# Row factors of an encoder layer's groups through memory, with TensorE's first microseconds laid out anew

## The chip, the cores and the metric

The kernel runs on one core of a Trainium2 chip. Its five engines run side by side and each takes its own instructions strictly in order: TensorE (PE) multiplies matrices, VectorE (DVE) and ScalarE (ACT) work elementwise, GpSimd (POOL) does slower elementwise work, and SyncE (SP) issues the DMA transfers, which 16 DMA engines carry out. The metric is the device time of the program in microseconds, smaller being better. The kernel before took 1175.03 us, the median of three runs (1173.93 to 1175.19).

## The reference

One hybrid encoder layer on x (4096 tokens, 1024 channels, float32):

```python
h = rmsnorm(x, pre_norm_g)                    # row factor = rsqrt(mean(x*x) + eps)
proj = einsum('bsd,de->bse', h, w_in)         # 1024 x 2304: q | k | v | g_a | u_p | g_p
a = banded_attention(q, k, v, rel_bias, sink) * silu(g_a)     # |i - j| <= 128
p = multiscale_pool(u_p, pool_w, pool_scale) * silu(g_p)
mixed = concat([a, p]) @ w_out
x = x + rmsnorm(mixed, post_norm_g)
```

The part that matters here is the first line: every token has one factor, and every channel of that token is multiplied by it before the projection. The bias of the attention is a table (32 buckets, 8 heads) that is spread over 512 relative positions.

## The kernel before

The work has two stages. Stage A (0 to about 500 us of the span) makes the gates and the pooled values (g_p, u_p, g_a); stage B makes q, k, v, the attention and the output. Float32 products are carried by pairs of float16 numbers: each operand is split in a high part (ACT copies it to float16) and a low part (DVE subtracts), and a product is three float16 matmuls.

Stage A handles the 4096 tokens in eight groups of 512, m = 0 to 7. Channels lie on the partitions, tokens along the free dimension, so a token's factor has to stand on all 128 partitions. For a group m the steps are (`prepare`, from line 933): four loads of x by token, four squares with row sums on ACT (`square`, L316), the power -1/2 on POOL (`root`, L304), which leaves the factors as a tile `rs` of 128 x 4; then on TensorE `spread_all` (L413): four float32 matmuls of `rs` against the identity, after which the factor of token t stands in column t of the PSUM tile `bc` on every partition. For each of four channel pairs the transposed x is loaded into `nt`, DVE multiplies it with `gsc` and `bc` (`norm`, L307), ACT and DVE split the result into `xb` and, for sums of quarters, `xt` (L446, L464, L304). The products (`y`, `x`, `v`, L634) follow; each result leaves its PSUM bank through an ACT copy (L742, L740) and a DVE addition (`cc`, `ubuf`).

Group 0 has a path of its own at the start of the kernel, for which the rest waits. Its x comes channel-major in 16 loads of 128 KB (`xb<-in_xT`, rows of 1 KB), for its first 256 tokens u = 0 and then for u = 1. ACT squares the four chunks of u = 0 (L387), DVE adds them up, TensorE sums over the partitions (`first_sum`, L398, into `sp`), DVE and POOL make the factors, TensorE spreads them (`bc`, L413), and DVE multiplies (`xb<-xb,gsc,bc`, L307). Beside it DVE needs the largest gain (`gain_most`; `gain_spread`, L370, on TensorE; the chain from L374 to `gh`), and the first weights need their column norms: ACT squares a weight tile (L519), TensorE sums it (`w_norm`, `n2ga` and `n2gb`, L528), DVE turns that into scales (`w_scale`, seven short instructions from L188), and ACT and DVE split the weights (L557, L307 `wq`). Only then do the products `plain` start: for half the channels with weight quarter A11, then A12, then for the other output half A21 and A22.

In stage A the order on every engine is set by a planner, `Steps.run`. A step has an engine, an estimated duration, a due time (`key`), the keys it reads and writes, and an assumed DMA time. The planner plays the steps through with these estimates: at each point it takes, on the engine that can start first, the ready step with the smallest due time. The result is a fixed order; on the chip nothing is reordered. So an edit to one step's due time or keys can move many others. Stage B has an order written out by hand, with times of its own (`plan`).

Attention's bias row is made once at about 267 us: `row_load` (two small DMAs), `row_prod` (a 32 x 512 float32 matmul, `fp`, L1009), `row_keep` (a DVE copy, L1013), `row_store`, and `bias_rows`, which spreads it through DRAM.

Of the kernel before, what the change touches and what calls it, by code (L numbers as in the profile page):

```python
# [17 lines left out]
P = 128  # L18
# [3 lines left out]
T = 512  # L22
# [34 lines left out]
class Steps:  # L57
# [28 lines left out]
    def run(self):  # L86
# [9 lines left out]
        free = dict.fromkeys(("PE", "DVE", "ACT", "POOL", "SP"), 0.0)  # L96
# [38 lines left out]
def hybrid_layer(ctx: ExitStack, tc, io, out):  # L135
# [40 lines left out]

    f_row = dram.tile([NH, 512], F32, name="f_row")
# [32 lines left out]
    with ExitStack() as actx:  # L210
# [12 lines left out]
        rs4 = pa.tile([P, 4], F32, name="rs4")  # L223
        xn1 = pa.tile([P, D], F32, name="xn")
# [115 lines left out]
        n0 = flat32(XB1).rearrange("p (k b t) -> p k b t", k=HK, b=2)  # L340
# [5 lines left out]
        for u in range(2):  # L346
            for c in range(HK):
                for b in range(2):
                    ld(-9 + 5 * u + 0.1 * c, n0[:, c, b, tok(u)], xT[c][:, b, 0, tok(u)], 0.13,
                       w=[f"n0.{c}.{u}.{b}"])  # L350
            if u == 0:
                ld(-8.75, g_pre, io["g_pre"], 0.02, w=["gpre"])
                ld(-8.74, ident, io["ident"], 0.06, w=["ident"])
            for i in range(2):
                w_load(GP, 2 * u + i, -8 + 5 * u)
# [24 lines left out]
        do("PE", 0.3, -6, gain_spread, r=["ident", "gmost"], w=["bc"])  # L380
# [5 lines left out]
        def first_square(c):  # L386
            A.activation(xsq[:, c], n0[:, c, :, tok(0)], AF.Square, scale=X_SQ)  # L387
# [34 lines left out]

        def n_view(m, c):
            if m == 0:
                return n0[:, c]
            return NT[:, (c % 2) * D : (c % 2 + 1) * D].rearrange("p (b t) -> p b t", b=2)

        def norm(m, c, b, ts=slice(0, T)):
            n = n_view(m, c)[:, b, ts]
            k = HK * b + c  # L430
            stt(n, n, gsc[:, k : k + 1], bc[m][:, ts], ALU.mult, ALU.mult)

        def norm_half(c, u):
            for b in range(2):
                norm(0, c, b, tok(u))
# [5 lines left out]
        def b_in(m, c, u=None):  # L441
            n = n_view(m, c)
            return n.rearrange("p b (u t) -> p b u t", u=2) if u is None else n[:, :, tok(u)]
# [4 lines left out]
        def b_low(m, c, u=None):  # L448
            tt(V, b_out(m, c, 1, u), b_in(m, c, u), b_out(m, c, 0, u), ALU.subtract)
# [26 lines left out]
        do("PE", 0.9, -4, first_sum, r=["onesf", "xsq3"], w=["wup1"])  # L476
# [6 lines left out]
        for u in range(2):  # L483
# [3 lines left out]
            for c in range(HK):  # L487
                do("DVE", 0.85, k + 0.5 * c, norm_half, c, u,
                   r=["gs"] + [f"bc{i}" for i in (2 * u, 2 * u + 1)]
                   + [f"n0.{c}.{u}.{b}" for b in range(2)],  # L490
# [3 lines left out]
                do("DVE", dve(512), k + 0.5 * c + 0.2, b_low, 0, c, u,  # L494
# [107 lines left out]
        norms([13, 13], 13, [tile_view(GP, i) for i in (2, 3)], [tile_keys(GP, i) for i in (2, 3)],  # L602
# [14 lines left out]
        do("DVE", 0.2, 20, gp_gates, r=["swga", "swgb"], w=["gates"])  # L617
        do("DVE", 1.2, 40, gp_flags, r=["swga", "swgb", "gates"], w=["flags", "swgc"])
        plain_weights(GP, (sw[:, 0:1], sw[:, 2:3]), ("ga", "gb"), (9.5, 12.5, 16.0, 17.0))
# [312 lines left out]

        def prepare(m):
# [7 lines left out]
            do("POOL", 1.0, key + 3, root, m, slice(0, 4), r=[f"ssq{m % 2}.{i}" for i in range(4)] + ["mhalf"],  # L941
               w=["rs4", "rs0", "rs1"])
            do("PE", 1.2, key + 5, spread_all, m, r=["rs4", "ident"], w=[f"wup{m % 2}"])
            for c in range(HK):
# [4 lines left out]
                for h in range(2):  # L949
                    do("DVE", dve(512), k + h, norm, m, c, h, r=["gs", f"wup{m % 2}"], w=[n])  # L950
# [48 lines left out]
        row_t = {}  # L999

        def row_load():
            row_t["b"] = pa.tile([32, NH], F32, name="rbias")
            nc.sync.dma_start(row_t["b"], io["rel_bias"])
            row_t["o"] = sqt[0].bitcast(F32)[:32]
            nc.sync.dma_start(row_t["o"], io["onehot"])

        def row_prod():
            row_t["p"] = psa.tile([NH, 512], F32, name="fp", tag="n20")
            nc.tensor.matmul(row_t["p"], row_t["b"], row_t["o"], start=True, stop=True)  # L1009

# [13 lines left out]
        def row_steps(key):  # L1024
            do("SP", 0.9, key, row_load, w=["row", "sqt0"], dma=0.3)
            do("PE", 1.8, key + 5, row_prod, r=["row", "sqt0"], w=["rowp", "n20"])
            do("DVE", 0.7, key + 8, row_keep, r=["rowp"], w=["n20", "rows", "sqt1"])
            do("SP", 0.45, key + 10, row_store, r=["rows", "sqt1"], w=["frow"], dma=0.1)
            do("SP", 0.45, key + 20, bias_rows, r=["frow"], w=["fscr"], dma=4.0)
# [1065 lines left out]
```

## Time and profile before

| | |
|---|---|
| time, median of 3 runs | 1175.03 us |
| time of the profiled execution | 1174.91 us |
| its span (first to last instruction) | 1172.8 us |
| PE busy | 1149.0 us (98%) |
| DVE busy | 930.8 us (79%) |
| ACT busy | 702.6 us (60%) |
| POOL busy | 309.3 us (26%) |
| DMA moved | 224.65 MB, mean 192 GB/s |

The profile was taken in one execution. A busy time is a sum over the span, and an engine that is busy all the time in one stage and idle in another has the same share as one that is half busy throughout, so the stretches are read one by one. In the timeline rows a group of like instructions has its start, the time until the last one's end, and behind the bracket the idle time ahead of it with what ended that. Matmuls are pipelined: a row's time holds the tail of its last matmul, so the distance to the next row's start is what the engine was occupied.

### The profile page before, as it was taken

Reading aid. Unit: us, or ns where it says so; the run is one execution under the profiler, and the core shown is the slowest. Engines: PE = TensorE matmul, PEld = TensorE weight load, DVE = VectorE, ACT = ScalarE, POOL = GpSimd, SP = SyncE. Lnnn points to the kernel's source line nnn. Section 1 sums busy time; section 2 is a strip of 40 time slices with the busy share of each in tenths; the row PEclk is TensorE's granted clock in tenths of the full one; section 3 lists DMA queues with packets and bytes.
Section 4 is the critical chain, followed back from the end, with each engine's and each line's share of the span. In section 5 each row is a group of like instructions: output and inputs, shape, how many; then the busy total and the mean of one; then the engine's idle time right before and its main releaser. Section 6 shows DMA issues by size and latency. Waiting matters only on the chain.

```text
span 1172.8 us, 33945 instructions
## 1 busy us (share of the span) xinstructions
PE 1149.0 (98%) x14304; PEld 883.4 (75%) x14304; DVE 930.8 (79%) x1865; ACT 702.6 (60%) x1459; POOL 309.3 (26%) x310
## 2 busy tenths in 40 slices
PE   5999999999999999999999999999999999999997
PEld 4998888888888888986667667576676667767653
DVE  6889997868788984558878878877887787887787
ACT  5875565546655552256676666666667666666672
POOL 0002111101101100201434434433533443443331
PEclk9999999999999999999999999999999999999999
DMA  8645488666756565299976886786777678687695
GB/s 315 218 111 169 162 261 268 185 234 221 255 189 232 153 186 176 56 279 209 263 184 140 191 198 133 197 196 159 182 193 185 142 190 200 136 194 160 164 234 144
DMA packets 292441, 224.65 MB, mean 192 GB/s; under 512 B 210704, under 2 KB 251920, under 8 KB 287680
## 3 DMA queue, kind: packets, MB, share of 16 engines
q1 hardware_dynamic: 292288, 222.48, 69.8%
q8 instruction: 112, 1.84, 0.6%
q14 instruction: 41, 0.34, 0.1%
HBM read 113.37 MB, written 60.33 MB: 148 GB/s over the span
## 4 chain that ended last, share of the span: by engine, by line
PE 50%; DVE 1%; ACT 0%; issue 0%; DVEq 0%; POOLq 0%; ACTq 0%
PE ms L1588 13%; PE aq L1227 12%; PE m L1588 9%; PE s L1272 4%; PE kv L1373 3%; PE o L1438 3%; PE kv L1227 3%; PE p L1438 2%; PE z L1560 1%; PE s L1560 0%; DVE pn L1336 0%; DVE mo L1627 0%; DVE p L1295 0%; ACT pn L1328 0%; DVE xt L1649 0%
## 5 line engine op out<-in xcount | busy, mean ns | idle before, releaser
L634 PEld LDWEIGHTS <-wq 128*128 128x128 f16 x4104 | 401.5, 98 | 52.7 <-issue 2.8
L634 PE MATMUL y<-xt,wq 128*128 128x256 f16 x1512 | 204.2, 273 | 0.9 <-ACT cc L742 0.9
L1306 ACT ACTIVATE p<-p,nm 128x385 f32<-128x385 f32 (+1 forms) x256 | 152.8, 599 | 35.0 <-POOL p L1289 20.3
L1227 PE MATMUL aq<-xb,xb 128*128 128x256 f16 x1024 | 173.4, 273 | 0.1
L1588 PE MATMUL ms<-wo,ys 128*128 128x512 f16 x720 | 162.7, 379 | 0.1
L1336 DVE SCALAR_TENSOR_TENSOR pn<-p,rd,pn 128x384 f16<-128x384 f32 (+1 forms) x256 | 156.1, 660 | 6.8 <-ACT pn L1328 6.8
L1295 DVE CUSTOM_DVE_ANT_0 p<-s,nt,nsink 128x384 f32<-128x384 f32 (+1 forms) x256 | 155.9, 665 | 1.8 <-PE s L1272 1.7
L1227 PEld LDWEIGHTS <-xb 128*128 128x128 f16 x1280 | 125.1, 98 | 22.8 <-issue 6.6
L1227 PE MATMUL aq<-xb,xt 128*128 128x256 f16 x512 | 139.6, 273 | 0.1
L1328 ACT ACTIVATE pn<-p,rd 128x384 f16<-128x384 f32 (+1 forms) x256 | 134.4, 596 | 4.2 <-issue 1.1
L1588 PEld LDWEIGHTS <-ys 128*128 128x128 f16 x720 | 69.2, 98 | 81.4 <-issue 2.8
L304 POOL TENSOR_TENSOR yt<-yt,sg 128x512 f32<-128x512 f32 (+2 forms) x32 | 48.0, 1499 | 311.4 <-DVE yt L307 293.1
L1588 PE MATMUL m<-wo,y 128*128 128x512 f16 x540 | 121.8, 379 | 0.0
L1588 PEld LDWEIGHTS <-y 128*128 128x128 f16 x540 | 51.5, 98 | 62.9 <-issue 2.9
L1622 POOL TENSOR_TENSOR mo<-mo,gpost 128x512 f32<-128x512 f32 x39 | 63.8, 1635 | 94.7 <-ACT jkb L1611 93.5
L634 PE MATMUL plain<-xb,wq 128*128 128x256 f16 x576 | 68.8, 276 | 3.0 <-ACT xb L446 1.8
L1227 PEld LDWEIGHTS <-xt 128*128 128x128 f16 x640 | 62.6, 98 | 8.3
L634 PE MATMUL y<-xb,wq 128*128 128x256 f16 x504 | 68.8, 273 | 0.0
L634 PE MATMUL v<-xb,wq 128*128 128x256 f16 x504 | 68.6, 273 | 0.2 <-DVE cc L304 0.2
L634 PE MATMUL v<-xt,wq 128*128 128x256 f16 x504 | 68.6, 273 | 0.0
L634 PE MATMUL x<-xb,wq 128*128 128x256 f16 x504 | 68.3, 273 | 0.0
L1272 PE MATMUL s<-k_all,q 64*32 64x288 f16 (+7 forms) x3648 | 62.5, 266 | 1.3 <-issue 1.3
(212 smaller groups left out, 1907.8 us busy)
## 6 DMA issues: line engine op xcount, KB each, us to landing
nt<-in_xT SPq DMA_DIRECT2D x28, 512.0 KB, 4.7
x_scr<-xb SPq DMA_DIRECT2D x14, 1024.0 KB, 7.2
xb<-x_scr SPq DMA_DIRECT2D x14, 1024.0 KB, 7.3
xr<-in_x SPq DMA_DIRECT2D x28, 512.0 KB, 4.6
out<-xr SPq DMA_DIRECT2D x28, 512.0 KB, 2.6
xn<-in_x SPq DMA_DIRECT2D x27, 512.0 KB, 4.4
ga_scr<-cc SPq DMA_DIRECT2D x64, 128.0 KB, 2.1
raw<-in_w_out SPq DMA_DIRECT2D x16, 512.0 KB, 5.4
```

What stands on the lines that cost most here:

```text
L304: eng.tensor_tensor(out=out, in0=in0, in1=in1, op=op)
L634: nc.tensor.matmul(b[:, s], wq[:, slot[q, op], wv, s, k, :], x[:, xv, k, :], start=(first and k + s + wv + xv == 0), stop=(last and k == H ...
L1227: nc.tensor.matmul(acc, w[:, j, k, :], x[:, kh, v, kt, :], start=(n == 0), stop=(n == 3 * KT - 1),)
L1272: nc.tensor.matmul(s_ps[qs, gg, c0:c1], q_t[u, half][a, qi, jj, tl + 32 * hq : tl + 32 * hq + 32], k_all[a, ki, kc + c0 - s0 : kc + c1 - s ...
L1295: nc.vector.tensor_tensor_reduce(out=p_t[b, half][:, hh, :nk], in0=s_t[jj][:, gg, :nk], in1=bias[:, h, lo : lo + nk], scale=negc[:, h : h ...
L1306: nc.scalar.activation(p[:, hh, : nk + 1], p[:, hh, : nk + 1], AF.Exp, bias=nm_t[b, half][:, hh : hh + 1], scale=-1.0, accum_out=den_t[b, ...
L1328: nc.scalar.activation(prob_view(b, half)[:, 0, i], p_t[b, half][:, i, :nk], AF.Copy, scale=rd_t[b, half][:, i : i + 1],)
L1336: nc.vector.scalar_tensor_tensor(out=pn4[:, 1, i], in0=p_t[b, half][:, i, :nk], scalar=rd_t[b, half][:, i : i + 1], in1=pn4[:, 0, i], op0= ...
L1373: nc.tensor.matmul(av[:, i], x[:, kh, v, kt, i * P : (i + 1) * P], w[:, B_V, k, :], start=(n == 0), stop=(n == 3 * KT - 1),)
L1438: nc.tensor.matmul(o_t[b][side][a, half], v_t[ku][ks, vi, kt, a], pt[b, half][ks, pi, g, :, kb - kbs[0], (LOW, TOP)[side]], start=start, s ...
L1588: nc.tensor.matmul(z_t[u, tag], y[:, k, yi, :], wo[o][:, wi, k, :], start=(n == 0 and acc is None), stop=(n == 3 * HK - 1), skip_group_che ...
L1622: eng.tensor_tensor(out=mo, in0=mo, in1=gpost[:, cs], op=ALU.mult)
```

## The change

Five things are changed. For the groups m = 3 to 7 the spread on TensorE is replaced: `rows_store` writes the 128 x 4 factors to 512 consecutive float32 numbers in DRAM (elements of 4 bytes), `rows_load` reads them back onto all 128 partitions as the SBUF tile `rows`, and `norm` reads that in place of `bc`; the loads, squares and the root of these groups get due times 16 us earlier, and two steps on a made-up engine "NET" tell the planner 12 and 7 us for the two transfers. The first x comes from a host-side copy `x0` in eight loads of 256 KB with rows of 2 KB. Filler matmuls (`turn_over`: `ones` times `ones`, into a bank that nobody reads) stand on TensorE: 52 ahead of `gain_spread`, 40 behind it, 24 behind the first weight scales. `first_sum` is forced ahead of the first weight norms by the key "summed". The bias row's product moves from 267 us to the start, its copy from DVE to ACT. Some steps of the first weights change their due times and keys. `LOW0` is empty, so no low part moves to POOL.

```diff
+        def row_keep():
+            row_t["s"] = row_t["o"][:NH]
+            A.copy(row_t["s"], row_t["p"])
...
+        do("SP", 0.9, -4.5, row_load, w=["row", "yt0"], dma=0.3)
+        n0 = flat32(XB1).rearrange("p (k u b t) -> p k u b t", k=HK, u=2, b=2)
...
-                for b in range(2):
-                    ld(-9 + 5 * u + 0.1 * c, n0[:, c, b, tok(u)], xT[c][:, b, 0, tok(u)], 0.13,
-                       w=[f"n0.{c}.{u}.{b}"])
+                ld(-9 + 5.5 * u + 0.1 * c, n0[:, c, u], io["x0"][u, c], 0.25, w=[f"n0.{c}.{u}"])
...
-                w_load(GP, 2 * u + i, -8 + 5 * u)
+                w_load(GP, 2 * u + i, -8 + 4 * u)
...
-        do("PE", 0.3, -6, gain_spread, r=["ident", "gmost"], w=["bc"])
+        def turn_over(n):
+            t = psa.tile([P, 2, 2 * P], F32, name=f"idle{n}", tag="v")
+            for _ in range(n):
+                nc.tensor.matmul(t[:, 0, :P], ones16, ones16, start=True, stop=True,
+                                 skip_group_check=True)
+
+        do("PE", 5.5, -9, turn_over, 52, r=["ones"], w=["bankv", "turned"])
+        do("PE", 0.3, -6, gain_spread, r=["ident", "gmost", "turned"], w=["bc", "spread0"])
+        do("PE", 2.3, -6, turn_over, 40, r=["ones", "spread0"], w=["bankv"])
...
+        def rows_store(m):
+            nc.sync.dma_start(rs_scr[m].rearrange("(i p) -> p i", i=4), rs4)
+
+        def rows_load(m):
+            bc[m] = rows
+            nc.sync.dma_start(
+                rows, rs_scr[m].rearrange("(o t) -> o t", o=1).to_broadcast([P, T])
+            )
...
-        do("PE", 0.9, -4, first_sum, r=["onesf", "xsq3"], w=["wup1"])
+        do("PE", 0.5, -4, first_sum, r=["onesf", "xsq3"], w=["wup1", "summed"])
...
-                do("PE", 0.5, key + 0.5, w_norm, z, group, i, n, b, r=["ones", f"sqt{z}"],
-                   w=[f"n2{b}"])
+                do("PE", 0.5, key + 0.5, w_norm, z, group, i, n, b,
+                   r=["ones", f"sqt{z}"] + ["summed"] * (group == "ga"), w=[f"n2{b}"])
...
+        do("PE", 1.4, 6, turn_over, 24, r=["ones", "swga"], w=["bankv"])
+        do("PE", 0.9, 5.6, row_prod, r=["row", "yt0", "summed"], w=["n20"])
+        do("ACT", 0.7, 5.6, row_keep, w=["n20", "yt0"])
+        for i, op, key in ((0, A11, 9.5), (1, A12, 12.5)):
+            pair(GP, op, i, sw[:, 0:1], key, "ga")
...
-        do("DVE", 0.2, 20, gp_gates, r=["swga", "swgb"], w=["gates"])
+        do("DVE", 0.2, 20, gp_gates, r=["swga", "swgb"] + [f"xb0.{c}.1l" for c in range(HK)], w=["gates"])
...
+            early = 16 * (m >= MS)
...
-                t = key - 9 + 3 * i if m > 1 else 20 + i
+                t = key - 9 - early + 3 * i if m > 1 else 20 + i
...
-            do("PE", 1.2, key + 5, spread_all, m, r=["rs4", "ident"], w=[f"wup{m % 2}"])
+            if m < MS:
+                spread_key = f"wup{m % 2}"
+                do("PE", 1.2, key + 5, spread_all, m, r=["rs4", "ident"], w=[spread_key])
+            else:
+                spread_key = "rsp"
+                do("SP", 0.6, key - 12, rows_store, m, r=["rs4"], w=["rs_scr"])
+                do("NET", 12.0, key - 12, lambda: None, w=["rs_scr"])
+                do("SP", 0.45, key - 8, rows_load, m, r=["rs_scr"], w=["rsp"])
+                do("NET", 7.0, key - 8, lambda: None, w=["rsp"])
...
-                    do("DVE", dve(512), k + h, norm, m, c, h, r=["gs", f"wup{m % 2}"], w=[n])
+                    do("DVE", dve(512), k + h, norm, m, c, h, r=["gs", spread_key], w=[n])
...
-            do("DVE", 0.7, key + 8, row_keep, r=["rowp"], w=["n20", "rows", "sqt1"])
...
+        "x0": np.ascontiguousarray(
+            x2[:T].reshape(2, UT, 2, HK, P).transpose(0, 3, 4, 2, 1)
+        ),
```

What this does to the order is seen at three places. The first is TensorE around the sum over the partitions of group 0 (`sp<-onesf,nt`; `n2ga` are the norms of the first two weight tiles, `sq` their squares). Before:

```order
L528 LDWEIGHTS ones_71
L528 MATMUL n2ga<-sq_116,ones_71 128x128
L398 MATMUL sp_197<-onesf,nt 128x1 x2
L528 LDWEIGHTS ones_71
L528 MATMUL n2ga<-sq_115,ones_71 128x128
```

In the changed kernel, at the sum and then six rows from a little later (`idle` is the filler's bank, `fp` the bias row's product, `bc` the spread of the factors of u = 0):

```order
L404 LDWEIGHTS ones_71
L404 MATMUL idle_221<-ones_71 128x128
L427 MATMUL sp_284<-onesf,nt 128x1 x2
L568 LDWEIGHTS ones_71
L568 MATMUL n2ga<-sq_118,ones_71 128x128
```

```order
L568 LDWEIGHTS ones_71
L568 MATMUL n2ga<-sq_118,ones_71 128x128
L352 MATMUL fp<-yt_121,rbias 8x512
L442 MATMUL bc_278<-ident,rs_114 128x128 x2
L568 LDWEIGHTS ones_71
L568 MATMUL n2ga<-sq_117,ones_71 128x128
```

The sum stood behind the eight matmuls of the first weight norm; now it stands ahead of them, behind the fillers, and the bias row's product stands between it and the spread.

The second place is DVE from the sums of squares of group 0 on (`nt` holds the squares, `ssq` is the row sum, the seven rows from `m<-n2ga` to `isc` are the weight scales, `xb<-xb,gsc,bc` the multiplication by the factors, two rows for each channel chunk). Before:

```order
L304 TENSOR_TENSOR nt<-nt 128x512 x2
L304 TENSOR_TENSOR nt<-nt 128x256
L296 TENSOR_SCALAR ssq_117<-sp_197 128x2
L188 TENSOR_REDUCE m_214<-n2ga 128x1
L194 TENSOR_SCALAR m_216<-m_214 128x1
L199 TENSOR_SCALAR m_218<-m_216 128x1
L203 TENSOR_SCALAR m_218<-m_218 128x1
L208 TENSOR_SCALAR sw<-m_218 128x2
L296 TENSOR_SCALAR sc<-sw,gh 128x2
L536 RECIPROCAL isc<-sc 128x2
L307 SCALAR_TENSOR_TENSOR xb_68<-xb_68,gsc,bc_178 128x256 x4
L307 SCALAR_TENSOR_TENSOR wq<-wq,sw 128x1024
```

In the changed kernel:

```order
L306 TENSOR_TENSOR nt<-nt 128x512
L306 TENSOR_TENSOR nt<-nt 128x256
L298 TENSOR_SCALAR ssq_119<-sp_284 128x2
L309 SCALAR_TENSOR_TENSOR xb_68<-xb_68,gsc,bc_278 128x256 x2
L189 TENSOR_REDUCE m_332<-n2ga 128x1
L195 TENSOR_SCALAR m_334<-m_332 128x1
L200 TENSOR_SCALAR m_336<-m_334 128x1
L204 TENSOR_SCALAR m_336<-m_336 128x1
L209 TENSOR_SCALAR sw<-m_336 128x2
L298 TENSOR_SCALAR sc<-sw,gh 128x2
L576 RECIPROCAL isc<-sc 128x2
L306 TENSOR_TENSOR xb_66<-xb_68,xb_66 128x2x256
```

The first chunk's multiplication moved ahead of the weight scales.

The third place is the DMA queue of SP where the factors of group 3 go out and come back (`rs_scr` is the new DRAM tensor, `raw` weights of stage B, `nt` and `xn` x, `ga_scr` and `yp_scr` results). The kernel before has neither row; in the changed kernel:

```order
L131 DMA xn<-in_x 128x1024
L453 DMA rs_scr<-rs_114 128x4x1
L131 DMA raw<-in_w_b 128x1024
L131 DMA nt<-in_xT 128x2x512
L131 DMA xn<-in_x 128x1024
L717 DMA ga_scr<-cc_124 128x2x128 x2
L881 DMA yp_scr<-yt_121 128x8
L882 DMA yp_scr<-yt_121 128x3x128
L887 DMA yp_scr<-yt_121 128x120
L457 DMA rows<-rs_scr 128x512
```

Between the store and the load that depends on it stand eight other issues.

## Rows read from the trace of the kernel before

**Rows 1.** Busy time by stretch: us, busy of each engine (instructions), PEclk, DMA share, GB/s.

```profile
0.00:19.11 19.11, 5.40 (x29) 4.07 (x30) 9.22 (x32) 9.87 (x13) 1.09 (x6) 1.00 0.82 269
19.11:22.90 3.79, 3.79 (x27) 3.13 (x26) 3.79 (x7) 3.56 (x6) 0.00 (x0) 1.00 1.04 401
...
125.00:150.00 25.00, 25.00 (x232) 22.43 (x230) 24.43 (x31) 16.04 (x23) 2.84 (x2) 1.00 0.50 161
...
153.00:500.00 347.00, 347.00 (x3203) 310.81 (x3202) 266.65 (x416) 171.85 (x241) 43.17 (x36) 1.00 0.64 201
```

**Rows 2.** Waits of PE from 60 to 560 us: total us, times, longest.

```profile
PE y L634 <- ACT cc L742: 0.9, 1, 0.9
```

**Rows 3.** Timeline of PE at the start: start, us, instruction, count, idle before and releaser.

```profile
11.34 1.01 PE L528 MATMUL n2ga<-sq,ones 128*128 128x128 bf16 x8 [3.61 <-ACT sq L519]
12.15 0.96 PE L398 MATMUL sp<-onesf,nt 128*128 128x1 f32 x4
...
14.14 1.22 PE L413 MATMUL bc<-ident,rs 128*128 128x128 f32 x4 [0.16 <-POOL rs L304]
...
22.05 1.06 PE L528 MATMUL n2gb<-sq,ones 128*128 128x128 bf16 x8
22.90 3.12 PE L634 MATMUL plain<-xb,wq 128*128 128x256 f16 x24
25.86 0.61 PE L413 MATMUL bc<-ident,rs 128*128 128x128 f32 x4
26.30 6.72 PE L634 MATMUL plain<-xb,wq 128*128 128x256 f16 x60
```

**Rows 4.** Timeline of SP's queue at the start.

```profile
0.72 2.77 SPq L131 DMA_DIRECT2D xb<-in_xT  x6
```

**Rows 5.** Timeline of ACT at the start: squares of the first and last chunk.

```profile
3.52 0.63 ACT L387 ACTIVATE nt<-xb 128x512 f32<-128x512 f32 x1 [1.30 <-DMA xb<-in_xT]
...
7.81 0.63 ACT L387 ACTIVATE nt<-xb 128x512 f32<-128x512 f32 x1 [1.56 <-DMA xb<-in_xT]
```

**Rows 6.** Timeline of DVE at the start.

```profile
7.77 0.29 DVE L374 TENSOR_REDUCE m<-sp 128x1 f32<-128x128 f32 x1 [1.52 <-PE sp L370]
...
9.05 1.87 DVE L304 TENSOR_TENSOR nt<-nt 128x512 f32<-128x512 f32 x3
13.14 0.16 DVE L296 TENSOR_SCALAR ssq<-sp 128x2 f32<-128x2 f32 x1 [2.23 <-PE sp L398]
14.02 0.42 DVE L188 TENSOR_REDUCE m<-n2ga 128x1 f32<-128x256 f32 x1 [0.72 <-PE n2ga L528]
...
15.60 1.66 DVE L307 SCALAR_TENSOR_TENSOR xb<-xb,gsc,bc 128x256 f32<-128x256 f32 x4
17.17 1.28 DVE L307 SCALAR_TENSOR_TENSOR wq<-wq,sw 128x1024 f16<-128x1024 f32 x1
...
23.54 0.42 DVE L188 TENSOR_REDUCE m<-n2gb 128x1 f32<-128x256 f32 x1
...
26.30 2.47 DVE L307 SCALAR_TENSOR_TENSOR wq<-wq,sw 128x1024 f16<-128x1024 f32 x2
```

**Rows 7.** Timeline of PE at the spread of group 3.

```profile
151.70 1.16 PE L413 MATMUL bc<-ident,rs 128*128 128x128 f32 x8 [0.33 <-POOL rs L304]
152.69 0.82 PE L634 MATMUL y<-xt,wq 128*128 128x256 f16 x6
```

**Rows 8.** Timeline of PE at the bias row's product.

```profile
267.01 1.02 PE L1009 MATMUL fp<-sq,rbias 32*8 32x512 f32 x2
```

**Rows 9.** Timeline of PE at the spread of group 7.

```profile
324.03 1.06 PE L413 MATMUL bc<-ident,rs 128*128 128x128 f32 x8
324.92 0.82 PE L634 MATMUL y<-xt,wq 128*128 128x256 f16 x6
```

**Rows 10.** DMA issues by tensor: count, KB each, median us from issue to landing.

```profile
gb<-ga_scr SPq DMA_DIRECT2D x32, 256.0 KB, 4.4
...
yp_scr<-yt SPq DMA_DIRECT2D x28, 4.0 KB, 1.6
```

More of the change, by code (lines that the diff above doesn't have):

```diff
@@ L95, in run @@
         begun = [None] * n_steps
-        free = dict.fromkeys(("PE", "DVE", "ACT", "POOL", "SP"), 0.0)
+        free = dict.fromkeys(("PE", "DVE", "ACT", "POOL", "SP", "NET"), 0.0)
         dma_free = 0.0
@@ L223, in hybrid_layer @@
         rs4 = pa.tile([P, 4], F32, name="rs4")
+        rows = pa.tile([P, T], F32, name="rows")
         xn1 = pa.tile([P, D], F32, name="xn")
@@ L441, in b_in @@
         def b_in(m, c, u=None):
-            n = n_view(m, c)
-            return n.rearrange("p b (u t) -> p b u t", u=2) if u is None else n[:, :, tok(u)]
+            if u is not None:
+                return n0[:, c, u]
+            return n_view(m, c).rearrange("p b (u t) -> p b u t", u=2)
+        LOW0 = ((), ())
         def b_high(m, c, u=None):
@@ L448, in b_low @@
         def b_low(m, c, u=None):
-            tt(V, b_out(m, c, 1, u), b_in(m, c, u), b_out(m, c, 0, u), ALU.subtract)
+            tt(G if u is not None and c in LOW0[u] else V, b_out(m, c, 1, u), b_in(m, c, u), b_out(m, c, 0, u), ALU.subtract)
         ts = NT[:, 2 * D : 3 * D].rearrange("p (o t) -> p o t", o=4)
@@ L471, in hybrid_layer @@
             do("ACT", act(512), -5 + 0.1 * c, first_square, c,
-               r=[f"n0.{c}.0.{b}" for b in range(2)], w=[f"xsq{c}", f"n0.{c}.0"])
+               r=[f"n0.{c}.0"], w=[f"xsq{c}"])
         for c, d in ((0, 1), (2, 3), (1, 3)):
@@ L488, in hybrid_layer @@
                 do("DVE", 0.85, k + 0.5 * c, norm_half, c, u,
-                   r=["gs"] + [f"bc{i}" for i in (2 * u, 2 * u + 1)]
-                   + [f"n0.{c}.{u}.{b}" for b in range(2)],
+                   r=["gs"] + [f"bc{i}" for i in (2 * u, 2 * u + 1)],
                    w=[f"n0.{c}.{u}"])
@@ L493, in hybrid_layer @@
                    w=[f"xb0.{c}.{u}h"])
-                do("DVE", dve(512), k + 0.5 * c + 0.2, b_low, 0, c, u,
+                e, us = ("POOL", 1.4) if c in LOW0[u] else ("DVE", dve(512))
+                do(e, us, k + 0.5 * c + 0.2, b_low, 0, c, u,
                    r=[f"n0.{c}.{u}", f"xb0.{c}.{u}h"], w=[f"xb0.{c}.{u}l"])
@@ L615, in gp_flags @@
             t_scalar(V, uf, sc[:, 0:1], U_EVAC * GP_EVAC * H_SCALE, ALU.mult)
-        do("DVE", 0.2, 20, gp_gates, r=["swga", "swgb"], w=["gates"])
+        do("DVE", 0.2, 20, gp_gates, r=["swga", "swgb"] + [f"xb0.{c}.1l" for c in range(HK)], w=["gates"])
         do("DVE", 1.2, 40, gp_flags, r=["swga", "swgb", "gates"], w=["flags", "swgc"])
-        plain_weights(GP, (sw[:, 0:1], sw[:, 2:3]), ("ga", "gb"), (9.5, 12.5, 16.0, 17.0))
+        for i, op, key in ((2, A21, 16.0), (3, A22, 17.0)):
+            pair(GP, op, i, sw[:, 2:3], key, "gb")
         bank_t = {}
@@ L937, in prepare @@
                 xn, k = (xn1, "xn") if m > 1 or i % 2 == 0 else (NT[:, 2 * D : 3 * D], "ts")
[L938 removed]
+                t = key - 9 - early + 3 * i if m > 1 else 20 + i
                 ld(t - 3, xn, x_blk[BPM * m + i], 0.5, w=[k])
                 do("ACT", 1.3, t, square, m, i, xn, w=[k, f"ssq{m % 2}.{i}"])
[L941 removed]
+            do("POOL", 1.0, key + 3 - early, root, m, slice(0, 4), r=[f"ssq{m % 2}.{i}" for i in range(4)] + ["mhalf"],
                w=["rs4", "rs0", "rs1"])
[L943 removed]
+            if m < MS:
[7 more added lines that the diff above has]
+                do("NET", 7.0, key - 8, lambda: None, w=["rsp"])
             for c in range(HK):
```

55 lines of the change are left out of this document (25 added, 30 removed).

## The prediction

> **What bounds the kernel now.** I read the busy times by stretch first. In [rows 1] PE is busy for 5.40 us of the first 19.11, and from 19.11 on it has hardly a gap: all 347.00 us from 153 to 500 are full. So whatever PE no longer does in that stretch comes off the end, and whatever brings the start of the steady stream forward does too; nothing else counts. The waits of PE confirm it: the longest one between 60 and 560 us is 0.9 us, for an ACT copy [rows 2]. But DVE is busy for 24.43 of 25 us from 125 to 150 [rows 1]: it is a near second there, and an edit that made it later would show.
>
> Then I read the start row by row, to see what the first products wait for. The fourth chunk of x lands last and its square starts at 7.81 [rows 5]. DVE is then in the gain chain (7.77 to 9.05), adds the squares until 10.92 [rows 6], and PE could sum them, but stands in the first weight norm: it starts that at 11.34 and comes to the sum at 12.15 [rows 3]. The row sum is on DVE at 13.14, the spread starts at 14.14, and DVE multiplies from 15.60 on, after the weight scales (14.02 to 15.60, 1.58 us) [rows 3, 6]. From 15.60 DVE has no idle until 23.54, when the last low part of x is done: 7.94 us of work. PE's stream is steady from 22.90; 12 + 24 products are done at 25.86, two spreads follow, and 12 more products at 0.109 us (6.72 us for 60, less the tail of the last) end the first 48 at 27.61 [rows 3].
>
> The profiled execution took 1174.91 us, 2.1 more than its span of 1172.8; the median of the three runs is 1175.03, so the sum below, made against 1174.91, can be read against the median as it stands.
>
> **Part 1: the spreads of groups 3 to 7 leave PE.** The first of the five occupies PE from 151.70 to 152.69, 0.99 us [rows 7], the last from 324.03 to 324.92, 0.89 us [rows 9]. Five of them are 4.45 to 4.95 us; I take 4.6. There is a further wait of 0.33 us ahead of the first, for POOL [rows 7], which I leave in the range. PE has no gap in that stretch, so the whole of it is gained, if `rows` is there in time. DVE's multiplication costs the same reading `rows` as reading `bc`. The price of the trip is not in the trace. The store has 512 pieces of 4 bytes. The nearest row is the 4 KB store in 128 pieces of 32 bytes, 1.6 us [rows 10]: four times the pieces give at least 1.6 and at most 6.4 us. The load of 256 KB costs what `gb` costs, 4.4 us [rows 10]. The trip is then 6 to 11 us by these rows (I take 7), against 16 us by which loads, squares and root are moved ahead. So I cost it at nothing; the cover is those 16 us, and without them DVE would stand at the multiplication. The added SP issues (two for each group, ten in all) lie beside PE, and the queue behind the load waits for the store's landing only.
>
> The Trainium skill (DMA: Bandwidth & Descriptors, Specifications) says that below 512 bytes a piece the DMA engine does read-modify-write; by that the store would be nearer to the upper figure above, and the sum would stay, since even that is under 16 us. No row before shows pieces of 4 bytes.
>
> **Part 2: the bias row's product leaves 267 us.** Its two passes take 1.02 us with a tail that the spread rows put at 0.17 (1.06 shown, 0.89 to the next row) [rows 8, 9]: 0.85 us gained. At the start it stands between the sum and the spread, where PE is otherwise waiting for DVE and POOL. It also takes its copy off DVE.
>
> **Part 3: the start.** SP issues the first six loads of 128 KB at 0.46 us each from 0.72 [rows 4]; the second half of the first chunk, issued at 1.18, has landed at 3.5 [rows 5], 2.3 us later. Now one issue brings 256 KB: at the 401 GB/s that the DMA engines reach from 19.11 on [rows 1], the first chunk lands at 0.72 + 2.3 + 0.3 = 3.3, and each next one 0.65 later, so the fourth at 5.3 in place of 7.8. Bounds: 5.0, if issuing alone sets it, and 7.8, if nothing changes; I take 5.3, as the source of the gap (eight issues, with two others between) is halved. Its square ends at 5.95, and DVE then has one addition (0.6), the gain chain (1.28), one addition and the fold (1.0): 8.9, if the gain's product is ready by 6.6.
>
> That is where the fillers matter. PE runs at the lower of its two levels at first: eight norm matmuls of 128 columns from 11.34 take until 12.15, 0.10 us each (1.2 GHz), and the last eight of `n2gb` still 0.85 us; from 26.30 a product of 256 columns takes 0.109 us (2.4 GHz) [rows 3]. The column PEclk says 1.00 in both stretches of [rows 1], so the level is read from the spacing. The rise lies near 22.90, after a stretch without a gap from 19.11. 52 fillers from 1.1 us at 0.106 take until 6.6 if all are slow; the rise should come within them, as it did in the stretch from 19.11. I take 6.0, and the 40 behind then end before 8.9. The sum starts at 8.9 in place of 12.15; from sum to spread 1.99 us as before, and the spread 0.61 as at 25.86 [rows 3]. Of the 1.99, one is DVE and POOL; `n2ga` (0.45) and `fp` (0.85) fill it and run over by 0.3, which a sum at the higher level gives back. DVE multiplies from 11.5 in place of 15.60.
>
> From there DVE does the same work plus the weight scales that it used to do ahead of it: 7.94 + 1.58 = 9.5 us, to 21.0. PE by then has 18 products; 30 more (3.3 us) and two spreads (0.44) take it to 24.8. DVE meanwhile needs the second weight scales (1.6), one multiplication of a pair (0.8), a wait for its spread (0.4) and the low part of A21 (2.47 for two, 1.24) [rows 6]: 25.0. So the first 48 products and their successor's weights are done at 25.0, in place of 27.61: 2.6 us gained, one for one with the start of the multiplication. The 24 later fillers wait for the weight scales (13.9) and end before the first product (17.4).
>
> **The sum.** 4.6 + 0.85 + 2.6 = 8.05 us: 1174.91 - 8.05 = 1166.9 us. DMA, squares and weights shift with the start, and stage B follows PE; its order is unchanged.
>
> **The rivals.**
> (a) PE's clock falls in the holes. In the new start PE stands idle between 12 and 14, 15 and 17, and 19 and 21 us. If it drops back to 1.2 GHz there, the stream starts slow, as from 19.11 to 22.90, where 3.79 us of busy PE [rows 1] did what half of that does later. Price 1.9 us: 1168.8. For it: the row at 14.14 still shows a slow spread (1.22 against 0.61) after 4 us of near steady work; against it, the holes are short and now follow long work. The Trainium skill (TensorE: Matmul & The Clock Gate, What's actually happening) says that the throttled state is the default and activity releases it; idle brings it back. The trace agrees on the rise; no row before shows a fall after it.
> (b) The fillers stand in the way. If the clock does not rise in them, the gain product ends at 7.4, the fold at 9.7, the 40 fillers at 11.7; sum, norm (0.8) and bias product (1.7) at the slow level bring the spread to 15.4 and the multiplication to 16.6, 5.1 us later than forecast: 1174.91 - 2.95 = 1172.0. Against it: the rise seen after 19.11.
> (c) The 2 KB rows do nothing, and the fourth chunk lands at 7.8: the fold then ends at 10.1, the multiplication starts 1.2 us later: 1168.1.
> (d) `rows` comes late, the one that ends slower. DVE works in order: a multiplication that waits for `rows` holds the additions (`cc`, `ubuf`) behind it, for whose banks PE waits. It decides from a trip of 16 us on; each us above costs five. At 18.1 us the kernel is slower; at a trip of 20 it is 1166.9 + 20 = 1186.9. Against it stand the 6 to 11 us above; for it, that no row shows 4-byte pieces, and that SP's queue is in order.
> (e) A new order always moves PE's small waits: 0.9 at an ACT copy and 0.33 at POOL may go or double, 1.2 us each way. That belongs to the forecast's own range.
>
> **How the numbers follow.** The forecast, 1166.9 (1164.6 to 1168.2 with (e) and the bounds of the spreads), has 0.60; (a) 0.20; (b) 0.08; (c) 0.07; (d) 0.05. The range for 8 in 10 takes in the forecast, (a), (c), and (a) with (c) but leaves out (b) and (d): 1164.6 to 1170.4. A difference of 0.2%, 2.35 us, is about what a measurement can tell from none. Faster by more than that (below 1172.7): the forecast, (a), (c), and half of (b) whose spread reaches over it, 0.91; within 0.2%: the other half of (b) and a small part of (d), 0.05; slower: (d), 0.04.
>
> **What would show it.** The fourth square starts near 5.3; the sum on PE near 8.9; DVE's first multiplication near 11.5; products at 0.109 us from about 21; the 12th of the second bank near 25. No PE gap where the five spreads and the bias product were; no DVE wait for `rows`. The prediction is wrong if the first products start no earlier than now, if their first 40 take 0.21 us each, or if DVE waits for `rows`.

## The result and the profile after

The changed kernel took 1178.39 us (median of five runs, 1175.56 to 1181.30), the kernel before 1175.03. The ratio is 1.0029, 95% interval 1.0018 to 1.0040: slower by 3.4 us, where 8.1 us faster was forecast. The profiled execution took 1181.30 us with a span of 1179.5, 6.7 longer than before's 1172.8; it is the slowest of the five, 2.9 us above the median, with the lowest mean granted clock of them (0.994 of full speed, the others 0.995 to 0.997), so its losses are larger than the median's.

The stretches that answer to [rows 1] show where (same columns):

```profile
0.00:19.11 19.11, 14.06 (x161) 12.09 (x162) 11.05 (x36) 13.07 (x17) 1.10 (x6) 0.99 0.94 324
19.11:22.90 3.79, 3.79 (x27) 3.04 (x26) 3.62 (x10) 1.99 (x6) 0.97 (x2) 0.60 1.02 416
125.00:150.00 25.00, 24.07 (x222) 21.35 (x220) 23.86 (x31) 14.09 (x21) 4.57 (x4) 1.00 0.78 178
153.00:500.00 347.00, 338.93 (x3089) 302.04 (x3088) 263.72 (x408) 166.55 (x231) 47.52 (x33) 0.99 0.72 198
```

From 153 to 500 us PE was full before; now 8.07 us of it are idle, and 0.93 more from 125 to 150. The waits of PE from 60 to 560 us, where [rows 2] had one of 0.9 (total, times, longest):

```profile
PE y L680 <- ACT cc L788: 2.6, 1, 2.6
PE v L680 <- issue: 2.0, 1, 2.0
PE y L680 <- ACT sg L712: 1.8, 1, 1.8
PE v L680 <- DVE cc L306: 1.6, 1, 1.6
...
PE tn L1023 <- ACT sq L1019: 0.9, 1, 0.9
```

None of them names `rows`. One goes back to it all the same, the gap of 1.6 us that ends on DVE's `cc`:

```profile
211.62 0.82 PE L680 MATMUL v<-xb,wq 128*128 128x256 f16 x6 [1.58 <-DVE cc L306]
```

DVE had been at work without idle since 206.59, where its longest wait for `rows` ended (its row stands below). The way to the cause of the others is to follow one of them back. PE around 234 to 244 us:

```profile
234.17 0.60 PE L680 MATMUL v<-xb,wq 128*128 128x256 f16 x4
236.80 0.38 PE L680 MATMUL v<-xb,wq 128*128 128x256 f16 x2 [2.03 <-issue]
237.02 1.35 PE L680 MATMUL y<-xt,wq 128*128 128x256 f16 x6
238.16 1.49 PE L680 MATMUL v<-xb,wq 128*128 128x256 f16 x6
239.44 1.37 PE L680 MATMUL y<-xt,wq 128*128 128x256 f16 x6
240.65 0.82 PE L680 MATMUL v<-xb,wq 128*128 128x256 f16 x6
243.30 0.82 PE L680 MATMUL y<-xb,wq 128*128 128x256 f16 x6 [1.83 <-ACT sg L712]
```

After the gap of 2.03 us, 18 matmuls take from 237.02 to 240.65, 3.63 us, where 18 take 1.97 elsewhere: the clock is at the lower level, and the fall costs another 1.66 us. A second fall follows the gap of 2.6 us (an ACT copy) that ends at 348.55; there 24 products take 4.28 us from 349.27 on, where 24 take 2.62 elsewhere, again 1.66 us. The Trainium skill (TensorE: Matmul & The Clock Gate, What's actually happening) says that idle brings the lower level back; these rows agree: the slow matmuls begin in the groups at 237.02 and 349.27, shortly behind the two gaps.

The gap of 1.83 us in the piece above has ACT behind it. The one of 2.03 us lies between two matmuls of one group, and the profile names nothing that ended it ("issue"); what held PE there stays open. ACT at that time:

```profile
241.53 1.06 ACT L1019 ACTIVATE sq<-raw 128x1024 bf16<-128x1024 f32 x1 [7.90 <-DMA raw<-in_w_b]
```

ACT works in order, and stood 7.90 us at a load of stage B's weights that has nothing to do with the row factors; the gate and the split of x queued behind it. Ahead of the gap of 2.6 us ACT stood at a DMA too, a store of results that had to land before its buffer was free:

```profile
347.91 0.59 ACT L788 COPY cc<-y 128x512 f32<-128x512 f32 x1 [5.15 <-DMA ga_scr<-cc]
```

The load of stage B's weights in the DMA issues (count, KB, median us to landing), with the two new transfers:

```profile
raw<-in_w_b SPq DMA_DIRECT2D x6, 512.0 KB, 14.5
...
rows<-rs_scr SPq DMA_DIRECT2D x5, 256.0 KB, 5.6
...
rs_scr<-rs SPq DMA_DIRECT2D x5, 2.0 KB, 10.3
```

In the kernel before the same load took:

```profile
raw<-in_w_b SPq DMA_DIRECT2D x6, 512.0 KB, 4.4
```

These medians are over the landings that the profile could tell: of the changed kernel two of the six loads (13.8 and 15.2) and one of the five stores, of the kernel before all six loads (3.6 to 9.1).

The load at 226.35 was issued 1.1 us behind the store of group 5's factors (225.27). What the DMA engines moved from 225.2 to 238.0 us, in 40 equal slices (busy share in tenths, then GB/s):

```profile
DMA  9897399999000990009090999705000272147997
GB/s 271 234 266 57 28 397 410 397 102 26 0 0 0 90 26 0 0 13 26 0 0 0 26 38 26 13 0 13 0 0 0 13 13 26 0 38 154 294 205 256
```

For some 8 us almost nothing moves, although many slices count as busy: the transfers in flight are stretched. It looks as if a store of 2 KB held up everybody's DMA; the experiments try that. The waits for DMA from 60 to 560 us, on all engines:

```profile
ACT sq L1019 <- DMA raw<-in_w_b: 16.1, 3, 7.9
...
DVE nt L309 <- DMA rows<-rs_scr: 3.8, 3, 2.5
```

In the kernel before ACT has no wait at `raw<-in_w_b` in this stretch. The wait for `rows` is there, but it is the small one. Its longest, for group 4, shows the whole trip, on SP and then on DVE:

```profile
181.01 0.37 SPq L453 DMA_DIRECT2D rs_scr<-rs  x1
...
193.54 0.32 SPq L457 DMA_DIRECT2D rows<-rs_scr  x1
```

```profile
206.59 1.41 DVE L309 SCALAR_TENSOR_TENSOR nt<-nt,gsc,rows 128x512 f32<-128x512 f32 x2 [2.47 <-DMA rows<-rs_scr]
```

25.6 us from store to multiplication, 9.6 more than the 16 by which the steps had been moved ahead.

At the start, PE (against [rows 3]):

```profile
1.07 4.95 PE L404 MATMUL idle<-ones 128*128 128x128 bf16 x52 [1.07 <-DVE ones L327]
...
9.52 0.58 PE L427 MATMUL sp<-onesf,nt 128*128 128x1 f32 x4 [0.52 <-DVE nt L306]
...
10.50 1.01 PE L352 MATMUL fp<-yt,rbias 32*8 32x512 f32 x2
11.44 0.71 PE L442 MATMUL bc<-ident,rs 128*128 128x128 f32 x4
...
15.40 0.28 PE L680 MATMUL plain<-xb,wq 128*128 128x256 f16 x1 [0.17 <-ACT wq L597]
18.03 1.93 PE L680 MATMUL plain<-xb,wq 128*128 128x256 f16 x11 [2.35 <-DVE wq L309]
19.76 1.06 PE L568 MATMUL n2gb<-sq,ones 128*128 128x128 bf16 x8
20.61 2.86 PE L680 MATMUL plain<-xb,wq 128*128 128x256 f16 x18
23.31 0.61 PE L442 MATMUL bc<-ident,rs 128*128 128x128 f32 x4
23.76 6.98 PE L680 MATMUL plain<-xb,wq 128*128 128x256 f16 x60
```

The clock is up at the sum (0.58 in place of 0.96), then falls after the gap of 2.35 us: `n2gb` takes 1.06 again, and PEclk is 0.60 from 19.11 to 22.90. The 37th product starts at 23.76 + 6 x 0.109 = 24.4, where before it started at 26.30: 1.9 us earlier.

The account up to the first product of stage B (`aq`, 497.26 before, 502.30 after: 5.0 us later): start -1.9, spreads -4.6, bias product -0.85; new gaps +9.0 less the 0.8 that went elsewhere (0.33 at the first spread, 0.45 from 100 to 125); two falls of the clock +3.3. That makes +4.2 of the 5.0. The other 1.7 us of the span arise in stage B, whose order is the same; I did not trace them. They need no cause in the change: from the first `aq` to the end the profiled executions of the later kernels take between 674.7 and 677.7 us (675.5 before, 677.2 here).

### The profile page after: what moved, and what is told of

Same layout as the page of the kernel before. It is cut to its first block, busy times and chain, and to the rows that moved or that the text cites. A ratio compares the mean times of both kernels' runs of the same rounds, so it can differ in the third digit from the quotient of the medians.

```text
span 1179.5 us, 34106 instructions
## 1 busy us (share of the span) xinstructions
PE 1154.3 (98%) x14380; PEld 887.0 (75%) x14380; DVE 933.3 (79%) x1864; ACT 702.3 (60%) x1460; POOL 315.8 (27%) x310
## 5 line engine op out<-in xcount | busy, mean ns | idle before, releaser
L306 POOL TENSOR_TENSOR yt<-yt,sg 128x512 f32<-128x512 f32 (+2 forms) x32 | 51.7, 1616 | 326.1 <-DVE yt L309 273.3
L1307 PE MATMUL s<-k_all,q 64*32 64x288 f16 (+8 forms) x3648 | 62.8, 266 | 1.8 <-issue 1.8
```

The costliest lines, as they stand in the source:

```text
L306: eng.tensor_tensor(out=out, in0=in0, in1=in1, op=op)
L1307: nc.tensor.matmul(s_ps[qs, gg, c0:c1], q_t[u, half][a, qi, jj, tl + 32 * hq : tl + 32 * hq + 32], k_all[a, ki, kc + c0 - s0 : kc + c1 - s ...
```

## Experiments

Theory T: the stores of 4-byte pieces hold up all DMA traffic, loads behind them come late, PE gets gaps and its clock falls. R1: the new order of steps makes the gaps. R2: only the wait for `rows` does. All were timed in five rounds or more.

**Spreads back on TensorE.**

```diff
-        MS = 3
+        MS = 8
```

> All groups are spread on TensorE again (MS = 8); the start, the fillers and the bias product stay as in the changed kernel. Theory T (the 512 pieces of 4 bytes of each store hold up the DMA engines for some 8 us, every load behind them lands late, TensorE gets gaps and its clock falls after the longer ones): no stores, no gaps after 100 us; the start's gain of 2.0 us and the bias product's 0.85 stay, so 1175.0 - 2.9 = 1172.2 us. Rival R1 (the new order of the steps, fillers and pairs makes the gaps, not the stores): gaps stay, 1177 to 1183. Rival R2 (the multiplication that waits for the factors alone makes them): as T, 1172.

1173.25 us, ratio 0.9986 (0.9977 to 0.9995). The gaps go (346.05 of 347 us busy from 153 to 500): what lost the time is in part 1. The rest of the change gains 1.5 us, not the 2.9 expected. The start has the order and the fillers of the changed kernel, and a gap of the same length, but in this execution the clock did not fall after it:

```profile
18.86 1.37 PE L680 MATMUL plain<-xb,wq 128*128 128x256 f16 x11 [2.35 <-DVE wq L309]
20.07 0.61 PE L568 MATMUL n2gb<-sq,ones 128*128 128x128 bf16 x8
```

So one profile does not give the start's worth. With this start the 37th product begins at 24.4 us in the changed kernel's profile, at 24.9 here, at 24.6 in the strided kernel's below, and at 26.9 and 26.5 in the four-token and the `MS = 2` kernels', where the clock fell; with the old start it begins at 26.3 to 27.2 (the kernel before and the three with unread stores).

**The store alone, in the kernel before.**

```diff
+    rs_scr = dram.tile([NM, T], F32, name="rs_scr")
...
+        def rows_store(m):
+            nc.sync.dma_start(rs_scr[m].rearrange("(i p) -> p i", i=4), rs4)
...
+            if m > 2:
+                do("SP", 0.4, key + 5, rows_store, m, r=["rs4"], w=["rs_scr"])
```

> The kernel before, every engine in its own order, with five stores of 512 pieces of 4 bytes added on SP's queue at the roots of groups 3 to 7; nobody reads them. T: loads behind them land some 8 us later, 1178 to 1185 us. R1 and R2: nothing waits for the store and the order is that of before, 1175.0, at most 1 us more.

1181.15 us, ratio 1.0054 (1.0040 to 1.0067): five stores of 2 KB that nobody reads cost 6.4 us. On the other four engines every instruction kept its place in the order, so R1 and R2 can't explain it. PE, full from 153 to 500 us before, has 3.4 us of idle time there, without a fall of the clock:

```profile
153.00:500.00 347.00, 343.61 (x3155) 306.90 (x3153) 265.36 (x415) 169.96 (x237) 42.02 (x33) 1.00 0.71 200
```

From 151 to 164 us, with the store issued at 152.91:

```profile
GB/s 416 403 148 260 292 454 423 454 429 429 403 403 302 378 454 454 378 353 504 302 277 176 151 22 154 290 309 214 25 25 19 25 57 69 38 50 57 57 63 69
```

The stall comes when the store's pieces reach their turn, behind the loads already queued.

**The same pieces, 512 bytes apart.**

The store-only kernel with two lines changed (shown against the kernel before):

```diff
+    rs_scr = dram.tile([NM, T, 128], F32, name="rs_scr")
...
+            nc.sync.dma_start(rs_scr[m].rearrange("(i p) z -> p i z", i=4)[:, :, 0:1], rs4.rearrange("p (i z) -> p i z", z=1))
```

> As the store added to the kernel before, but each of the 512 pieces of 4 bytes goes to an address 512 bytes from the next, so that no two share a short stretch of memory. If T holds by the number of pieces (each costs the same wherever it goes): as with the close addresses, 1178 to 1185 us. If T holds by pieces from different DMA engines into the same stretch of memory, which would have to wait for one another: 1175 to 1176 us.

1176.29 us, ratio 1.0011 (1.0002 to 1.0019); a store lands in 3.6 us (median of the three landings told, 2.0 to 7.1). Number and size of the pieces are the same, so most of the cost, 4.9 of 6.4 us, comes from their lying close together.

**Pieces of 16 bytes, close together.**

The store-only kernel with one line changed (shown against the kernel before):

```diff
+            nc.sync.dma_start(rs_scr[m].rearrange("(p i) -> p i", i=4), rs4)
```

> The kernel before with the five unread stores, now each in 128 pieces of 16 bytes instead of 512 of 4, into the same 2 KB. If what costs is many small pieces into the same short stretch of memory: a quarter of the pieces, about a quarter of the 6.4 us that the 4-byte stores cost, 1175.0 to 1176.6 us. If any store into so short a stretch costs the same whatever the size of its pieces: 1181 us.

1175.62 us, ratio 1.0007 (0.9998 to 1.0016). Same stretch, same bytes, same new DRAM tensor, a quarter of the pieces: a tenth of the cost (0.6 us), not clear of none. So it isn't the tensor's place in DRAM that costs. From 151 to 164 us:

```profile
GB/s 88 176 365 391 303 220 295 322 412 479 403 454 403 378 403 429 454 429 353 378 454 328 176 227 176 173 140 273 340 309 183 113 139 189 347 378 372 353 353 391
```

**The changed kernel with 16-byte pieces and a strided read.** Its order is that of the changed kernel.

```diff
-            nc.sync.dma_start(rs_scr[m].rearrange("(i p) -> p i", i=4), rs4)
+            nc.sync.dma_start(rs_scr[m].rearrange("(p i) -> p i", i=4), rs4)
...
-            bc[m] = rows
+            bc[m] = rows.rearrange("q (p i) -> q i p", i=4)
...
+            if m > 2:
+                n = n.rearrange("q (i p) -> q i p", i=4)
```

> The changed kernel in its own order, but the store is 128 pieces of 16 bytes (token order partition by partition) and DVE reads the loaded rows with a stride of 16 bytes. T: four times fewer pieces; the store lands like the 4 KB store of 128 pieces (about 2 us in place of 10.3), DMA keeps moving, the gaps of TensorE after 100 us (9.6 us) and the two falls of its clock (3.4) go: 1178.4 - 11 = 1167.5 us. R1: same order, so no change, 1178. R2: the trip is 8 us shorter, only the waits for the rows go (3.8 us in sum): 1174 to 1176.

1173.27 us, ratio 0.9988 (0.9979 to 0.9997): 5.1 us better than the changed kernel by the medians, 4.8 by the ratios, against R1, but short of T's 1167.5. DVE's 40 multiplications got dearer (min/median/max ns):

```profile
L309 DVE SCALAR_TENSOR_TENSOR nt<-nt,gsc,rows x40: 1126/1162/2197, 164.4 to 413.5; 128x512 f32<-128x512 f32 x40
```

They took 744 in the changed kernel; 40 x 0.42 = 17 us on an engine near its limit, and PE pays with a gap and a fall of the clock:

```profile
175.91 0.82 PE L682 MATMUL x<-xb,wq 128*128 128x256 f16 x6 [2.21 <-DVE ubuf L309]
```

**16-byte pieces without the stride.** Each partition takes four neighbouring tokens, by the order in which x is loaded for groups 3 to 7.

```diff
-            nc.sync.dma_start(rs_scr[m].rearrange("(i p) -> p i", i=4), rs4)
+            nc.sync.dma_start(rs_scr[m].rearrange("(p i) -> p i", i=4), rs4)
...
+        x4 = {(m, i): io["x"][m * T : (m + 1) * T].rearrange("(p i) d -> i p d", i=4)[i]
...
-                ld(t - 3, xn, x_blk[BPM * m + i], 0.5, w=[k])
+                ld(t - 3, xn, x_blk[BPM * m + i] if m < MS else x4[m, i], 0.5, w=[k])
```

> The changed kernel in its own order; for groups 3 to 7 a partition holds four neighbouring tokens (x is loaded in that order, rows of 4 KB as before), so the store is 128 pieces of 16 bytes and DVE reads the rows without a stride. Theory T (close 4-byte pieces hold up the DMA engines; in the 16-byte variant with strided reads what was left of the loss was DVE, 16 us more busy, with a gap of 2.2 us on TensorE and a fall of its clock worth 1.7): both causes are gone, 1173.3 - 4.2 = 1169 us, 1167.5 if all gaps seen in the changed kernel go. Rival R1 (the new order of the steps itself loses what the spreads give): 1173.

1169.25 us, ratio 0.9956 (0.9943 to 0.9968), as T said. DVE no longer waits for `rows`, and PE is nearly full again:

```profile
19.11:22.90 3.79, 2.43 (x15) 1.91 (x16) 3.79 (x7) 3.22 (x6) 0.00 (x0) 0.72 1.03 417
...
153.00:500.00 347.00, 346.27 (x3203) 310.48 (x3201) 271.63 (x424) 171.83 (x242) 48.90 (x36) 1.00 0.66 204
```

Against the spreads on TensorE the way through memory is now worth 4.0 us by the medians, 3.5 (0.30%) by the ratios; I had taken 4.6. The next six build on this kernel.

**Three fillers in place of 116.**

```diff
-            for _ in range(n):
+            for _ in range(1):
```

> As the four-token variant, but each of the three groups of fillers is one matmul instead of 52, 40 and 24. If the fillers bring the clock up early and that counts: the sum, norms, spread and the first products run at 1.2 GHz, the multiplication starts some 1 us later and the stream's first 3 to 4 us run at half speed: 1.5 to 2.5 us slower than with the fillers. If TensorE waits for DVE there anyway: within 0.7 us of it. If the fillers stand in the way: faster.

1171.35 us (0.9972, 0.9960 to 0.9983), 2.1 slower by the medians, with intervals that just overlap: the fillers are most likely worth their place. After 30 products the stream goes on at

```profile
27.09 5.12 PE L680 MATMUL plain<-xb,wq 128*128 128x256 f16 x43
```

so the 37th starts at 27.7, 1.4 us later than before: the rest of the new start, on a slow clock, loses.

**The first x in 1 KB rows.**

```diff
-                ld(-9 + 5.5 * u + 0.1 * c, n0[:, c, u], io["x0"][u, c], 0.25, w=[f"n0.{c}.{u}"])
+                def x0_load(c, u):
+                    for b in range(2):
+                        nc.sync.dma_start(n0[:, c, u, b], xT[c][:, b, 0, tok(u)])
...
```

> As the four-token variant, but the first x comes again in 16 loads of 128 KB with rows of 1 KB at the same places of the queue. If the loads set the first sum, as in the prediction: the fourth chunk lands at 7.5 to 7.8 in place of 5.3, DVE's last additions end 1.2 us later, the time is 1.0 to 1.5 us longer. If the gain chain sets it (it ends at 8.2 in the changed kernel, after the squares): the same time within 0.5 us.

1170.19 us (0.9962, 0.9950 to 0.9975): 0.9 us slower, just under the expected 1.0. The fourth square starts at 7.04 (5.68 in the changed kernel's profile, 6.41 in the four-token one's), so the 2 KB rows do bring x earlier; the intervals of the two ratios overlap, so what that is worth at the end is not settled.

**Group 2 through memory too** (`MS = 2`).

> As the four-token variant, with group 2 through memory too (MS = 2). T: one spread less on TensorE, 0.9 us faster than the four-token variant, 1167 to 1168. Rival: the steps 16 us earlier fall into the stretch from 60 to 125 us where DVE is nearly full (24.46 of 25 us), and the gap grows: no gain or slower.

1169.87 us (0.9957, 0.9943 to 0.9970): no gain by the medians. PE is busy for 48.72 of the 50 us from 150 to 200, in the four-token kernel for 49.27, so part of the spread saved comes back as a gap. Not all of it does: from the 37th product to the first `aq` this kernel's profile takes 464.9 us, the four-token one's 465.5, a gain of 0.6 that is lost in the scatter of the medians.

**Fillers in the gap.**

```diff
-do("PE", 1.4, 6, turn_over, 24, r=["ones", "swga"], w=["bankv"])
+do("PE", 1.4, 6, turn_over, 60, r=["ones", "swga"], w=["bankv"])
```

> As the four-token variant, but the third group of fillers is 60 matmuls instead of 24: 36 more at 0.0625 us are 2.2 us, which fill the 2.1 to 2.4 us in which TensorE waits for DVE's first low weights. If the falls of the clock seen in the stretch from 14 to 24 us come from that gap and cost: no fall there, the first 30 products at 0.109 us, 0.7 to 1.5 us faster than the four-token variant, 1168. If the start is set by DVE (one multiplication and low part after the other) whatever the clock: the same time within 0.4 us.

1168.55 us (0.9951, 0.9938 to 0.9963): 0.7 faster by the medians. Its profiled run shows slow norms at 13.90 all the same, after gaps of 0.4 to 0.5 us earlier on, so by itself it didn't show the clock held.

**Fillers in both gaps** (also 52 to 68).

> As the one with 60 fillers in the third group, and 68 instead of 52 in the first, to cover the 1.6 us that TensorE waits for the largest gain at about 7 us. If that wait brings the clock down too: a further 0.3 to 0.7 us faster. If the gain's sum over the channels comes at 6.3, as in the changed kernel, they delay it by 0.3 us: the same or 0.3 us slower.

1167.98 us (0.9947, 0.9934 to 0.9961), the lowest median: 6.6 us below the kernel before in the same runs (1174.58) and 10.4 below the changed one (9.6 by the ratios). In its profile the gap ahead of the eleven products is down to 0.76 us and the clock holds through the start (PEclk 1.00 where the four-token kernel had 0.72, `n2gb` 0.61):

```profile
19.11:22.90 3.79, 2.87 (x30) 2.31 (x29) 3.79 (x7) 2.86 (x6) 0.23 (x1) 1.00 1.03 420
```

```profile
18.90 1.38 PE L680 MATMUL plain<-xb,wq 128*128 128x256 f16 x11 [0.76 <-DVE wq L309]
20.11 0.61 PE L568 MATMUL n2gb<-sq,ones 128*128 128x128 bf16 x8
```

That the added fillers hold the clock is not shown by this: with 52 and 24 fillers at these two places it held too in the profiles of the kernel with the spreads back and of the strided one. The two filler versions' intervals overlap each other and the four-token kernel's; the order of the three medians is as expected, the sizes are not settled to half a microsecond.

**The bias product twice.**

```diff
             nc.tensor.matmul(row_t["p"], row_t["b"], row_t["o"], start=True, stop=True)
+            nc.tensor.matmul(row_t["p"], row_t["b"], row_t["o"], start=True, stop=True)
```

> As the four-token variant, but the bias row's product at the start is issued twice. If it stands in a hole, as the prediction says (TensorE waits for DVE and POOL between the sum and the spread): within 0.3 us of the four-token variant. If it is on the path to the spread: 0.9 us slower, and then the move gave nothing.

1169.25 us (0.9956, 0.9944 to 0.9969), the same as with one, but with an interval of 1.5 us to either side that doesn't settle 0.9. The profile tells more:

```profile
9.93 0.58 PE L428 MATMUL sp<-onesf,nt 128*128 128x1 f32 x4 [0.47 <-DVE nt L306]
...
10.98 1.01 PE L352 MATMUL fp<-yt,rbias 32*8 32x512 f32 x2
11.83 1.01 PE L353 MATMUL fp<-yt,rbias 32*8 32x512 f32 x2
12.78 0.71 PE L443 MATMUL bc<-ident,rs 128*128 128x128 f32 x4
```

From the sum to the spread it takes 2.85 us, in the changed kernel 1.92 (9.52 to 11.44): the second product pushes the spread by 0.93, and the products behind it by as much (the second one starts 9.44 us after the sum, 8.51 there). So the end of the product is on the path to the spread. With one product it is so by some 0.3 us: the changed kernel's factors leave POOL at 11.07, and the spread follows 0.37 later, where it followed 0.06 later before (14.08 and 14.14).

POOL in the changed kernel, then in the kernel before:

```profile
10.37 0.70 POOL L306 TENSOR_TENSOR rs<-ssq,mhalf 128x2 f32<-128x2 f32 x1 [9.45 <-DVE ssq L298]
```

```profile
13.38 0.70 POOL L304 TENSOR_TENSOR rs<-ssq,mhalf 128x2 f32<-128x2 f32 x1 [12.46 <-DVE ssq L296]
```

## Why the prediction was wrong

**Part 1, the step that failed.** "So I cost it at nothing; the cover is those 16 us, and without them DVE would stand at the multiplication." I asked only whether the trip would be back in time, and bounded the store from 1.6 us for 128 pieces of 32 bytes up to 6.4 by their number. The one landing that the profile tells came after 10.3. Worse, I priced the store as if it cost only those who wait for it; it cost every transfer queued with it. The store-only kernel puts that at 6.4 us in the old order, and the pieces set 512 bytes apart show that their closeness made most of it. The cover was nearly enough for the trip (DVE waited 3.8 us in sum) and no cover at all for the neighbours: ACT's 16.1 us at weight loads, DVE behind ACT, PE behind both, then the clock. One gap of PE, 2.0 us, has no cause that the profile names.

The rule that I weighed there (the Trainium skill, DMA: Bandwidth & Descriptors, Specifications: read-modify-write below 512 bytes) pointed to a dearer store, and the store was dearer. But piece size alone isn't it here: the same 4-byte pieces set apart landed in 3.6 us.

**Rival (d)** had the right sign, and its mechanism made the smaller part. Trips did pass 16 us (25.6 for group 4), but DVE's waits for `rows` sum to 3.8 us, three of them, where (d) wanted each us five times over. One of them did what (d) says: the gap of PE of 1.6 us at 210, out of 9.0, lies behind the wait of 2.47. It got 0.05, since I let it depend on that one wait.

**The value of the spreads** was about right: 4.6 forecast, 4.0 (3.5 by the ratios) once the store is cheap. The extra DVE cost "the same reading `rows` as reading `bc`" held without a stride: 744 ns.

**Part 2** held for the most part: the product stands mostly in a hole, but its end holds up the spread by some 0.3 us, which the prediction saw and thought to get back from a faster sum. A second product goes onto the path whole.

**Part 3** was mis-sized, 2.6 forecast, 1.9 in the profiled run, and some 0.6 by the medians of the kernel with the spreads back (1.5 less the bias product's 0.85). The sum came at 9.52 for 8.9, the multiplication at 12.19 for 11.5, and this was the best of the five profiles of this start: the fourth square began at 5.7 to 6.7 for 5.3, and the gain's product, which the sum wanted by 6.6, at 6.3 to 7.3. And rival (a), falls of the clock in the holes, happened in some executions and not in others: PEclk 0.60 from 19.11 to 22.90 here, 1.00 in the kernel with the spreads back. It was priced at 1.9; counted from the sum, the 37th product begins 14.5 and 14.9 us later in the two profiles without a fall and 14.9, 16.0 and 16.6 in the three with one, so a fall came with anything from nothing to some 2 us. Rivals (b) and (c) did not come about: the fillers help, by 2.1 us in the median, and the 2 KB rows bring x earlier.

## What to carry to other kernels

Price a transfer by what it does to the transfers beside it, not only by when it lands: look at the GB/s of the slices around it and at the landing times of the loads issued just behind it. When a small tile has to go through memory, choose the order of its elements so that each partition writes one run, and move the permutation to a load whose rows are long anyway. On an engine that is full, a gap costs its length and, as here, may cost a fall of the clock on top, so it is worth a try to fill the idle time in front of a stream that is about to start. And where such a fall comes in one execution and not in the next, price a start from several profiles and not from one.

## What the runs showed of the hardware

- 512 pieces of 4 bytes into 2 KB land in 10.3 us (one landing told) and let almost nothing else through for some 8 us (at 228 us of the changed kernel); 512 bytes apart they land in 3.6; 128 pieces of 16 bytes, close together, in 2.9 to 4.3 (medians of the strided, the four-token and the unread-store kernel). Why closeness matters (a queue at the memory or in the DMA engines) was not tried.
- A float32 operand of DVE read with a stride of 16 bytes makes a 128x512 multiplication 1162 ns in place of 744.
- Soon after gaps of 2.03, 2.35 and 2.6 us TensorE fell to half speed; after those of 1.6 us at 210 and 1.83 at 243 it did not, nor after one of 2.35 at the same place of the start in the profiles of the kernel with the spreads back and of the strided one. In the run with 60 fillers it fell at the start after three gaps of 0.4 to 0.5 us.
